# A list schedule that reckons with a transfer rate of 205 GB/s in place of 370 GB/s for all but the first nine DMA transfers of a two-layer encoder

## The chip, the cores and the metric

One core of a Trainium2 chip runs the whole kernel. The metric is the device time of one execution in microseconds, as the median of several executions.

## The reference

The input x (512 tokens by 1024) is layer-normed and goes through two layers. Each layer projects x with w_in (1024 x 4608) into three groups of heads, mixes them with w_out, norms, and then runs a gated MLP with a convolution of width 3. Cut to what matters:

```python
proj = x @ w_in                       # split into da_q, da_k, da_v, hg_q, hg_ff, hg_fb, hg_i, hg_g, mx_q
da_o = rms_norm(diff_attention(dq, dk, dv, lam), da_norm_g)          # 4 heads
hg_o = rms_norm(o_fwd + o_bwd, hg_norm_g) * silu(hg_g)               # gated linear recurrence, 4 heads
mx_o = memory_attention(mx_q, mem @ w_mem_kv)                        # 256 memory tokens, 4 heads
x = layer_norm(ALPHA * x + concat(da_o, hg_o, mx_o) @ w_out)
u = depthwise_conv_centred(x @ w_up, conv_w, conv_b)                 # 2 x 2816 channels
gate, val = split(u)
x = layer_norm(ALPHA * x + (silu(gate) * val) @ w_down)
```

All inputs and weights are float32.

## The kernel before

**Weights.** Every weight goes through `prep` in pieces of 1 MB, 122 in all. A piece is loaded by SyncE into a staging tile `wst` (two buffers); ScalarE squares it and sums (L307); TensorE adds the sums over the partitions in a matmul of one column (`stat`, L168); three small VectorE instructions make a power-of-two scale from it (L155, L157, L159); ScalarE writes the float16 high part `wh` (L310), VectorE the float16 low part `wl` (L311). `wh` and `wl` have four buffers each. After L311 the staging buffer is free for the next load. For w_up a piece is two loads of 512 KB (L300), for the others one load of 1024 KB (L302).

**Matmuls.** Every product is made of three float16 matmuls (high x high, high x low, low x high) in `mm` (L140), so one piece feeds 48 matmuls of 512 columns, but half as much for w_mem_kv, where there are 256 memory tokens. The PSUM tiles of the projections are called mm (two buffers) and sc (three), those of transposes and of small sums tr (two).

**The MLP.** The 22 pairs of gate and value columns are worked in groups of 2, 4, 4, 4, 4 and 4. A pair is 48 matmuls (mm: gate, sc: value), then for each half a ScalarE instruction out of PSUM (L1147) and two VectorE ones for the convolution (L1148, L1149), then the SiLU (L1150) and the product on GpSimd (L1151), which writes a quarter of the group's tile t. When the group is whole, `split_group` squares it on ScalarE (L536), sums it by a matmul of one column (`gss`, L168) and splits it into float16 high and low parts (L545, L547). While that happens TensorE multiplies the group before with w_down (`down`, with its results added to z by VectorE in L569). This place, where a group ends, is called a boundary below.

**The planner.** The instructions are first traced without an order. `make_plan` then makes one: `extract` gives each a cost in microseconds and its predecessors, `deadlines` a due time counted back from TensorE's program order (through buffer reuse too), and `simulate` runs a list schedule: on each engine the instruction that is ready first goes next, and of several ready ones the one with the earliest due time. Which instruction uses which buffer follows from the same simulation. The plan is then frozen: the kernel is built a second time with every engine's queue in exactly this order and with these buffers. The chip does not choose; each engine takes its queue from the front, and an instruction that waits holds up all behind it.

In `simulate` a transfer holds the memory for its bytes over `DMA_RATE`, one transfer after the other, and lands `DMA_LAT` = 2.1 us on top of that. In `deadlines` a load is due its bytes over `DMA_RATE` plus 2 us before its first reader. The first nine transfers of the program (`FIRST`: the constants, two rows of the first norm's vectors, four tiles of x, two weight pieces) get due times that put them ahead of everything.

Of the kernel before, what the change touches and what calls it, by code (L numbers as in the profile page):

```python
# [1205 lines left out]

LAT = 0.055
DMA_LAT = 2.1
DMA_RATE = 370e3


def _esize(dt):
# [72 lines left out]
def extract(instrs):  # L1285
    ops = []
    last_half = None
    for i in instrs:
# [3 lines left out]
        o = Op()  # L1292
# [96 lines left out]
    for o in ops:  # L1389
        for p in o.preds:  # L1390
            ops[p].succs.append(o.i)
    run = []
    for o in ops + [None]:
        if o is not None and o.eng != "PE":
# [12 lines left out]
def simulate(ops, tiles, prio, fixed=None, wait=0.0, log=None):  # L1407
# [65 lines left out]
    while done < N:  # L1473
# [42 lines left out]
        if o.dmab:  # L1516
            free[e] = t + o.cost
            d0 = max(dma_free, t + 0.3)
            dma_free = d0 + o.dmab / DMA_RATE
            end[i] = dma_free + DMA_LAT - 0.3  # L1520
# [25 lines left out]

PEN = 20.0
FIRST = 9


def deadlines(ops, tiles):
# [23 lines left out]
    for i in range(N - 1, -1, -1):  # L1575
        o = ops[i]
        d = T[i] if o.eng == "PE" else 1e9 if succ[i] else t
        for s in succ[i]:
            x = D[s] - o.cost - o.tail - LAT
            if o.dmab:  # L1580
                x -= o.dmab / DMA_RATE + 2
            d = min(d, x)
        D[i] = d
    for k, o in enumerate([o for o in ops if o.dmab][:FIRST]):
        D[o.i] = k - 1000.0
# [3 lines left out]
def make_plan(instrs):  # L1589
    ops, tiles = extract(instrs)  # L1590
    _, _, _, order, slot_of = simulate(ops, tiles, deadlines(ops, tiles))
    return list(order.values()), {tiles[t].source_name: s for t, s in slot_of.items()}
# [45 lines left out]
```

## Time and profile before

| what | us |
|---|---|
| median of 3 executions | 1530.62 (1529.3 to 1532.16) |
| the profiled execution, its own time | 1531.11 |
| its span | 1529.3 |
| TensorE busy in it | 1463.1 |
| VectorE busy | 1141.4 |
| ScalarE busy | 861.7 |

The profile is of one execution. Its span runs from the first to the last recorded instruction, and 1.8 us of its own time lie outside. TensorE's busy time is the union of its matmuls as recorded, whose ends are modelled: a matmul of 512 columns is listed with about 380 ns, though in a dense run one starts every 216 ns. A wait in brackets behind an instruction is the idle time of its engine just before it, with what ended it. "SPq" rows are SyncE's queue, which issues the transfers.

### The profile page before, as it was taken

The page shows a single profiled execution, that of the slowest core. Times are in us where ns is not written, and L with a number is a line of the kernel's source. Part 1 is how long each engine was busy: PE and PEld are TensorE (multiplying, and loading weights), DVE is VectorE, ACT ScalarE, POOL GpSimd, SP SyncE. Part 2 cuts the span into 40 slices and gives each one's busy share as a digit, 9 for nine tenths or more (in the row PEclk, how much of TensorE's full clock was granted, in tenths as well). Part 3 has the DMA queues.
Part 4 walks back from the last instruction along what each step waited for, and adds up shares of the span by engine and source line. Part 5 has one row for each costly group of instructions (what it writes and reads, how often), then busy time and mean ns, then how long its engine had stood idle before and what let it go on. Part 6 is the DMA issues. An engine that isn't in the chain of part 4 may idle for free. (4 is left out here: it accounts for less than half of the span.)

```text
span 1529.3 us, 24599 instructions
## 1 busy us (share of the span) xinstructions
PE 1463.1 (96%) x9978; PEld 813.2 (53%) x9978; DVE 1141.4 (75%) x2146; ACT 861.7 (56%) x1092; POOL 231.9 (15%) x250
## 2 busy tenths in 40 slices
PE   6999999998999999999999999999999999999997
PEld 4566575564474444444477476655556444444443
DVE  8998867967897576666685868678788677565767
ACT  6775556664375555545465646565745655545450
POOL 1221303030111000000110321122101101010111
PEclk9999999998999999999999999999999999999999
DMA  6432112212143232332333212121322334223221
GB/s 232 130 127 84 57 56 71 98 59 95 42 138 111 83 111 84 109 111 85 109 111 129 94 34 80 56 75 38 109 83 84 111 96 122 85 83 110 86 80 56
DMA packets 158172, 141.92 MB, mean 93 GB/s; under 512 B 3302, under 2 KB 139114, under 8 KB 158058
## 3 DMA queue, kind: packets, MB, share of 16 engines
q1 hardware_dynamic: 158058, 140.35, 28.2%
q8 instruction: 78, 1.28, 0.3%
q14 instruction: 36, 0.29, 0.1%
HBM read 138.24 MB, written 2.10 MB: 92 GB/s over the span
## 5 line engine op out<-in xcount | busy, mean ns | idle before, releaser
L311 DVE SCALAR_TENSOR_TENSOR wl<-wst,ws,wh 128x2048 f16<-128x2048 f32 x122 | 307.0, 2518 | 100.1 <-ACT wh L310 99.8
L140 PEld LDWEIGHTS <-wh 128*128 128x128 f16 x2624 | 250.8, 98 | 241.8 <-issue 8.1
L307 ACT ACTIVATE wh<-wst 128x2048 bf16<-128x2048 f32 x122 | 232.7, 1908 | 164.9 <-PE stat L168 48.6
L140 PE MATMUL mm<-xl,wh 128*128 128x512 f16 (+1 forms) x832 | 306.3, 368 | 0.0
L140 PE MATMUL mm<-xh,wh 128*128 128x512 f16 (+1 forms) x832 | 306.2, 368 | 0.1
L140 PE MATMUL mm<-xh,wl 128*128 128x512 f16 (+1 forms) x832 | 306.1, 368 | 0.0
L310 ACT ACTIVATE wh<-wst,ws 128x2048 f16<-128x2048 f32 x122 | 243.4, 1996 | 28.8 <-DVE ws L157 14.0
L140 PE MATMUL mm<-wh,t 128*128 128x512 f16 (+1 forms) x768 | 225.4, 370 | 2.7 <-DVE z L569 2.3
L140 PEld LDWEIGHTS <-wl 128*128 128x128 f16 x1312 | 128.5, 98 | 124.8 <-issue 2.3
L140 PEld LDWEIGHTS <-t 128*128 128x128 f16 x1152 | 110.1, 97 | 134.3 <-issue 15.5
L569 DVE SCALAR_TENSOR_TENSOR z<-mm,inv,z 128x512 f32<-128x512 f32 x176 | 129.9, 745 | 47.3 <-PE mm L140 34.3
L1151 POOL TENSOR_TENSOR t<-f 128x512 f32<-128x512 f32 x44 | 66.0, 1500 | 558.3 <-DVE f L1149 282.8
L140 PE MATMUL sc<-xh,wl 128*128 128x512 f16 (+1 forms) x416 | 147.4, 354 | 0.0
L140 PE MATMUL sc<-xl,wh 128*128 128x512 f16 (+1 forms) x416 | 147.4, 354 | 0.0
L140 PE MATMUL sc<-xh,wh 128*128 128x512 f16 (+1 forms) x416 | 147.4, 354 | 0.0
L140 PE MATMUL mm<-wl,t 128*128 128x512 f16 (+1 forms) x384 | 142.0, 370 | 0.0
L155 DVE TENSOR_SCALAR we<-stat 128x1 int32<-128x1 int32 x122 | 18.6, 152 | 94.4 <-PE stat L168 94.0
L140 PE MATMUL mm<-wh,mgh 128*128 128x512 f16 x192 | 73.8, 384 | 12.3 <-DVE z L569 12.3
L1150 ACT ACTIVATE f<-f 128x512 f32<-128x512 f32 x44 | 27.7, 630 | 83.2 <-DVE f L1149 74.6
L140 PE MATMUL mm<-wl,mgh 128*128 128x512 f16 x192 | 74.1, 386 | 0.0
L140 PE MATMUL mm<-wh,mgl 128*128 128x512 f16 x192 | 73.4, 383 | 0.7 <-DVE mgl L547 0.7
L1042 ACT ACTIVATE f<-sc,dam,iqk 128x512 f32<-128x512 f32 x64 | 49.2, 775 | 29.6 <-DVE dam L1040 29.6
(243 smaller groups left out, 2196.3 us busy)
## 6 DMA issues: line engine op xcount, KB each, us to landing
wst<-in_w_up_dram SPq DMA_DIRECT2D x88, 512.0 KB, 4.4
wst<-in_w_in_dram SPq DMA_DIRECT2D x36, 1024.0 KB, 4.9
wst<-in_w_down_dram SPq DMA_DIRECT2D x22, 1024.0 KB, 4.9
wst<-in_w_out_dram SPq DMA_DIRECT2D x12, 1024.0 KB, 4.8
wst<-in_w_mem_kv_dram SPq DMA_DIRECT2D x8, 1024.0 KB, 5.2
z<-in_x_dram SPq DMA_DIRECT2D x4, 512.0 KB, 4.5
mix<-in_ln_g_dram SPq DMA_DIRECT2D x4, 512.0 KB, 3.5
mix<-in_ln_b_dram SPq DMA_DIRECT2D x4, 512.0 KB, 4.8
```

The lines of the kernel that those rows point to most:

```text
L140: T.matmul(o, lhsT, rhs, start=start, stop=stop)
L155: V.tensor_scalar(e, tot.bitcast(I32), 0x7F000000, 1, ALU.bitwise_and, ALU.logical_shift_right)
L307: A.activation(h.rearrange("p a b -> p (a b)").bitcast(BF16), flat, AF.Square, accum_out=ss)
L310: A.activation(h.rearrange("p a b -> p (a b)"), flat, AF.Identity, scale=s)
L311: V.scalar_tensor_tensor(l.rearrange("p a b -> p (a b)"), flat, s, h.rearrange("p a b -> p (a b)"), ALU.mult, ALU.subtract)
L569: V.scalar_tensor_tensor(zs, p_, ivs[half % len(ivs)], zs, ALU.mult, ALU.add)
L1042: A.activation(pe[:, c, :], sc_[c], AF.Exp, bias=mx[:, c : c + 1], scale=iqk, accum_out=z1 if c else z0)
L1150: A.activation(c2[:, 0, :], c2[:, 0, :], AF.Silu)
L1151: G.tensor_tensor(gt[:, n, :], c2[:, 0, :], c2[:, 1, :], ALU.mult)
```

## The change

The planner's rate falls from 370e3 to 205e3 bytes per microsecond, and the sizes of the first nine transfers are scaled by 205/370 beforehand, so that for these the quotient stays what it was. All the others take 1.8 times as long in the plan, in the simulation and in the due times. No instruction is added or taken away; the four queues of the engines, SyncE's order of transfers and the choice of buffers are worked out anew from these numbers.

```diff
 LAT = 0.055
 DMA_LAT = 2.1
-DMA_RATE = 370e3
+DMA_RATE = 205e3
...
     for o in ops:
         for p in o.preds:
             ops[p].succs.append(o.i)
+    for o in [o for o in ops if o.dmab][:FIRST]:
+        o.dmab *= FAST
     run = []
...
 PEN = 20.0
 FIRST = 9
+FAST = 205 / 370.0
```

## Rows read from the trace of the kernel before

**Rows 1.** The page, part 1: busy time of each engine, share of the span, instructions.
```profile
PE 1463.1 (96%) x9978; PEld 813.2 (53%) x9978; DVE 1141.4 (75%) x2146; ACT 861.7 (56%) x1092; POOL 231.9 (15%) x250
```

**Rows 2.** The waits of TensorE over the whole span: who waited for whom, total us, how often, the longest.
```profile
PE mm L140 <- DVE z L569: 14.6, 11, 2.7
PE tr L262 <- DVE z L258: 9.0, 4, 4.9
PE tr L168 <- ACT t L536: 5.5, 4, 1.5
PE stat L168 <- ACT wh L307: 4.0, 7, 1.1
PE sc L140 <- POOL w L817: 3.7, 3, 1.9
```

**Rows 3.** The page, part 6: transfers by tensor, how many, KB each, median us from issue to landing.
```profile
wst<-in_w_up_dram SPq DMA_DIRECT2D x88, 512.0 KB, 4.4
wst<-in_w_in_dram SPq DMA_DIRECT2D x36, 1024.0 KB, 4.9
wst<-in_w_down_dram SPq DMA_DIRECT2D x22, 1024.0 KB, 4.9
```

**Rows 4.** The view of transfers over the first 60 us, in 40 slices of 1.5 us each: GB/s moved.
```profile
GB/s 0 59 251 393 421 398 386 385 387 426 391 410 346 0 0 261 384 172 129 0 30 0 0 136 386 178 57 350 292 0 0 11 0 5 67 357 382 368 206 18
```

**Rows 5.** The waits of SyncE's queue: total us, how often, the longest.
```profile
SPq L302 <- DVE wl L311: 833.0, 72, 28.9
SPq L300 <- DVE wl L311: 334.0, 37, 16.7
```

**Rows 6.** The waits of ScalarE over the whole span: total us, how often, the longest.
```profile
ACT wh L307 <- DMA wst<-in_w_up_dram: 36.4, 18, 4.2
...
ACT wh L307 <- DMA wst<-in_w_down_dram: 18.8, 8, 2.8
...
ACT t L536 <- POOL t L1151: 12.2, 4, 3.6
```

**Rows 7.** The timeline around one boundary in the MLP of the second layer (1338 to 1358 us): start us, duration us, engine, line, operation, out<-in.
```profile
1338.40 3.22 DVE L311 SCALAR_TENSOR_TENSOR wl<-wst,ws,wh 128x2048 f16<-128x2048 f32 x1 [0.35 <-ACT wh L310]
...
1343.40 0.63 ACT L1150 ACTIVATE f<-f 128x512 f32<-128x512 f32 x1 [1.66 <-DVE f L1149]
1345.88 0.17 PE L168 MATMUL stat<-wss,ones 128*128 128x1 bf16 x1
...
1347.01 1.91 ACT L307 ACTIVATE wh<-wst 128x2048 bf16<-128x2048 f32 x1 [2.97 <-DMA wst<-in_w_up_dram]
...
1348.91 0.76 ACT L1147 ACTIVATE f<-sc,cvb,cw 128x512 f32<-128x512 f32 x1
1349.06 0.16 PE L168 MATMUL stat<-wss,ones 128*128 128x1 bf16 x1 [0.61 <-ACT wh L307]
...
1349.58 1.99 ACT L310 ACTIVATE wh<-wst,ws 128x2048 f16<-128x2048 f32 x1
...
1351.69 2.35 DVE L311 SCALAR_TENSOR_TENSOR wl<-wst,ws,wh 128x2048 f16<-128x2048 f32 x1
1351.92 3.24 POOL L1151 TENSOR_TENSOR t<-f 128x512 f32<-128x512 f32 x1 [12.45 <-DVE f L1149]
...
1355.20 1.91 ACT L536 ACTIVATE t<-t 128x2048 bf16<-128x2048 f32 x1 [3.63 <-POOL t L1151]
...
1357.25 0.16 PE L168 MATMUL tr<-gss,ones 128*128 128x1 bf16 x1 [1.48 <-ACT t L536]
```

**Rows 8.** The view of one line, GpSimd's product in the MLP, over the whole span: duration ns min/median/max, first and last start us, shapes.
```profile
L1151 POOL TENSOR_TENSOR t<-f x44: 1264/1272/3304, 445.0 to 1481.6; 128x512 f32<-128x512 f32 x44
```

**Rows 9.** The same view of the low part of a weight on VectorE.
```profile
L311 DVE SCALAR_TENSOR_TENSOR wl<-wst,ws,wh x122: 2322/2351/3350, 19.1 to 1484.4; 128x2048 f16<-128x2048 f32 x122
```

**Rows 10.** Busy time by stretch, the first two of 50 us each and the last of 30 us (the span ends at 1529.3): PE, PEld, DVE, ACT, POOL busy us (instructions), granted clock of TensorE, share of the DMA engines, GB/s.
```profile
0.00:50.00 50.00, 36.05 (x219) 23.45 (x220) 42.69 (x108) 33.26 (x45) 3.88 (x14) 1.00 0.56 199
50.00:100.00 50.00, 47.35 (x592) 32.20 (x591) 44.64 (x97) 38.86 (x47) 11.81 (x9) 1.00 0.45 148
...
1500.00:1530.00 30.00, 19.92 (x93) 8.82 (x90) 22.40 (x36) 0.00 (x0) 6.11 (x8) 0.89 0.19 70
```

**Rows 11.** The timeline between 78 and 88 us, in the first layer's work on w_mem_kv: two L311 and the first matmul on TensorE with a weight of this stage behind each.
```profile
78.16 2.32 DVE L311 SCALAR_TENSOR_TENSOR wl<-wst,ws,wh 128x2048 f16<-128x2048 f32 x1
...
81.63 0.39 PE L140 MATMUL mm<-t,wh 128*128 128x256 f16 x2
...
84.33 2.35 DVE L311 SCALAR_TENSOR_TENSOR wl<-wst,ws,wh 128x2048 f16<-128x2048 f32 x1 [1.24 <-ACT wh L310]
...
87.19 0.28 PE L140 MATMUL mm<-wh,t 128*128 128x256 f16 x1
```

**Rows 12.** Busy time by stretch around 354 to 364 us, where the first layer's w_out stage ends: columns as in rows 10.
```profile
354.00:356.00 2.00, 0.92 (x6) 0.62 (x6) 2.00 (x5) 2.00 (x3) 0.00 (x0) 0.99 0.33 78
356.00:358.00 2.00, 1.26 (x6) 0.23 (x5) 2.00 (x7) 1.96 (x6) 0.00 (x0) 0.50 1.15 345
358.00:360.00 2.00, 2.00 (x8) 0.57 (x5) 2.00 (x3) 0.38 (x2) 0.00 (x0) 0.50 0.38 113
360.00:362.00 2.00, 2.00 (x7) 0.53 (x6) 0.95 (x7) 0.28 (x1) 0.00 (x0) 0.50 0.67 262
362.00:364.00 2.00, 2.00 (x13) 1.42 (x12) 1.53 (x6) 2.00 (x5) 0.00 (x0) 0.80 0.04 11
```

## The prediction

> **What bounds the kernel now.** I read the page's busy times first, then TensorE's waits, then the transfers and who waits for them, and last the timeline wherever TensorE stood still. TensorE is busy for 1463.1 us of 1529.3 [rows 1], so 66.2 us are idle, and no change of order can give more than that. Of these, 16.6 lie in the first 100 us (100 less 36.05 and 47.35) [rows 10], most of it waiting for the first norm, and 9.4 in the last 29.3 us (19.92 busy) [rows 10], where the last norm is stored; the planner can hardly touch either. Some 40 us are left, none of the waits longer than 2.7 us. The named ones [rows 2] are matmuls of the w_out and w_down stages that wait for L569 to empty a PSUM buffer (14.6), the gss matmul that waits for L536 (5.5 in 4), and the stat matmul that waits for L307 (4.0 in 7). None of TensorE's named waits is for a weight's low part, and SyncE sends a load as soon as L311 lets go of a staging buffer: that wait is nearly all its queue does [rows 5]. So transfers don't bound the kernel; the exact order in four in-order queues does.
>
> **Is the new rate the right one?** No. A piece of 1 MB costs the old plan 2.1 + 1.05 MB/370 GB/s = 2.1 + 2.83 = 4.93 us and the chip 4.9 [rows 3]; the opening burst runs at 385 to 425 GB/s [rows 4]. At 205 GB/s the plan reckons 2.1 + 5.11 = 7.21 us, 2.28 too much. A single half piece of w_up (4.4 [rows 3]) lies between the two plans' 3.5 and 4.7, but its second half follows at once: in [rows 7] an L311 that ends at 1341.6 frees the buffer, and ScalarE has the whole new piece at 1347.0, 5.4 us later with the issue. The change thus puts 2.28 us of slack behind each of some 120 loads. The Trainium skill, page "DMA: Bandwidth & Descriptors", section "Anatomy of one DMA — SWDGE (gpsimd) path", fits 2.0 us plus bytes over 436 GB/s to transfers that GpSimd issues; an estimate by that page is 4.4 us for 1 MB, the rows' 4.9 decides for these, and by the page the surplus would be 2.8 instead of 2.3, which speaks against the new rate as a description.
>
> **What the slack changes in the queues.** A due time only decides between instructions that are ready together, and a load is ready when its buffer is, which SyncE waits for anyway [rows 5]; so SyncE's order stays nearly the same, and so do the first nine loads. What moves is L307 on ScalarE. In the plan it is ready 2.28 us later, and whatever becomes ready in between goes ahead of it. The stat matmul on TensorE moves back with it. On the chip the data still come after 4.9 us, so neither is late for that reason.
>
> **Term 1, the stat matmul.** The old order, in which the data land just in time, leaves ScalarE idle before L307 for 36.4 + 18.8 us in 26 cases of the MLP [rows 6], and when the real landing is a little late, TensorE stands behind the stat matmul: 7 times, 4.0 us, 1.1 at most [rows 2]. All are shorter than 2.28, so a stat matmul that is planned 2.28 us later on TensorE finds its sum ready. I take -4.0 (bounds -4.0 and 0, where the matmul keeps its place for want of other work between). Late next is gss.
>
> **Term 2, the boundary.** The timeline of one boundary [rows 7] shows the whole chain. The last pair's sums are in PSUM at 1345.9, but the next in ScalarE's queue is L307, which waits 2.97 us for its load until 1347.01 and takes 1.91 more. L1147 behind it runs at 1348.91 instead of 1346; after it come the convolution, the SiLU, the product on GpSimd, L536 and gss, for which TensorE waits 1.48. With the slack, L1147 is ready some 2 us before L307 in the plan and goes first: 2.9 us gained in the chain of this boundary, more than the 1.48. Against that stands the product: it takes 3.24 us here beside an L311 [rows 7], where its median is 1.27 [rows 8] and the plan reckons about 1.4. L1147 first lets L310 of the older piece go next and L311 behind it, and L311 can meet the product again. Then 1.9 us of lateness remain, which alone would make the 1.48. I take half of the four waits, -2.7 (bounds -5.5 and 0). L311 is itself drawn out, 3.22 us [rows 7] against a median of 2.35 [rows 9]. The Trainium skill, page "GPSIMD Engine Reference", section "1. Specifications", says that GpSimd's access to SBUF is shared with VectorE, with contention beside instructions of two SBUF inputs; L311 is one, and the two durations in the rows agree. By that rule this term would be 0 and the sum 2.7 higher.
>
> **Term 3, the start.** Between 20 and 95 us each load is used almost as soon as it is ready: L311 ends at 80.48 and the next weight matmul starts at 81.63, another ends at 86.68 and TensorE uses it at 87.19 [rows 11], while VectorE is busy 42.69 and 44.64 of 50 us [rows 10]. Here w_mem_kv feeds only half as many matmuls per piece. An L307 that is queued later ends later, L311 too, and the staging buffer is reloaded later; nothing in VectorE's queue has room to make it good. What covers it is other matmuls (the recurrence), and where they run out TensorE waits. The price lies between 0 (cover holds) and two reuses of one buffer in this stretch, 2 x 2.28 = 4.6. I take 1.1, half of one reuse, as the rows show 0.5 to 1.2 us between the weight and its use and TensorE nearly always occupied.
>
> **Term 4, the rest.** The waits for L569 (14.6), for the recurrence's operands (3.7 for L817) and for norms [rows 2] are dealt out anew. No row gives a direction, so I take 0. For the bounds I take the dearest place that a wait of this kind now has: after a stretch in which TensorE was busy 0.92 and 1.26 of 2 us, its granted clock stands at 0.50, the 1.2 GHz level, from about 356 to 362.5 [rows 12]. Work done there takes twice as long, so some 6.5 us at that level cost about 3.3. One such fall more or less is -3.3 to +3.3.
>
> **Sum.** -4.0 - 2.7 + 1.1 + 0 = -5.6. The profiled execution took 1531.11, so its successor takes 1525.5; that execution stands 0.5 above the median of 1530.62, so the median comes to 1525.0.
>
> **Rivals.** *Nothing to measure.* The boundary keeps its waits because product and L311 meet (term 2 is 0), the start costs one whole reuse (+2.3), and two boundaries that now pass without a wait get the 1.48 (+3.0): -4.0 + 2.3 + 3.0 = +1.3, about 1532. The difference of 1.97 us between the product beside L311 and alone speaks for it (the rule of the Trainium skill under term 2 describes this case); that 8 of 12 boundaries have no gss wait now, though most have an L311 near, speaks against. That the change hardly does what it says belongs here too: if ScalarE has nothing else ready in the 2.28 us, the queues come out as they were, and the time is 1530.6. ScalarE's idle 36.4 us before L307 say that this is often so, but rows 7 that it isn't at the places that cost.
>
> *Slower: the weights of the start come late.* In the first 100 us, and again in the second layer's w_mem_kv and w_in pieces, the plan believes that two staging buffers give a piece only every 7 to 8 us and lets other work in front of L307. On the chip that work then really delays the reload, and the delay adds up over two reuses: +4.6, without gains at the boundaries, which makes 1535.2. It decides from the point at which TensorE's idle time in the first 100 us goes above some 20 us (16.6 now) and the waits name L310 or L311. For it: VectorE's load and the narrow margins of rows 10 and 11. Against: none of the costly waits names a weight today, and TensorE has the recurrence's matmuls to do.
>
> **How the numbers follow.** The forecast, 1525.0, has a chance of 0.50; nothing to measure 0.23; slower 0.27. Forecast's own range: 1520 (both terms whole, no cost at the start: -9.5 from 1530.6 is 1521, with part of a fall of the clock) to 1527.5. The whole range goes down to 1530.6 - 9.5 - 3.3, about 1518, and up to the slower case's 1535.2 with part of a fall of the clock, 1537. A measurement of this kernel can tell about 0.2%, 3.1 us, from no change; faster means below 1527.6, slower above 1533.7. Faster 0.50, same 0.23, slower 0.27.
>
> **What would show it.** Right: in TensorE's waits the line of stat behind L307 falls from 4.0 to under 1, the line of gss behind L536 from 5.5 to about 2.8; ScalarE's wait for w_up and w_down loads falls from 55 to under 30; at the boundaries L1147 of the last pair stands ahead of the L307 that waits for a load. Load durations stay at 4.9. Wrong: the idle time in the first 100 us grows by more than 4, the waits for L569 grow by more than the 6.7 of terms 1 and 2, or the clock stands at its lower level for longer in sum than before. I would be most wrong if the order of TensorE's own work (attention between projections) changes widely, for then the 40 us of small waits are dealt anew and term 4 outweighs the others.

## The result and the profile after

The changed kernel takes 1512.24 us (median of 4, 1509.85 to 1514.96) where the kernel before takes 1530.89 in the same comparison (median of 4): 0.988 times as long, 95% interval 0.986 to 0.990, or 18.6 us less. The forecast was 5.6 less. The profiled execution took 1512.29, with a span of 1510.5, so between the two profiled executions 18.8 us are gone.

The page, part 1 (busy time of each engine), and from part 6 the transfers, tensor by tensor, with the median from issue to landing:

```profile
PE 1458.8 (97%) x9978; PEld 816.0 (54%) x9978; DVE 1155.0 (76%) x2146; ACT 861.3 (57%) x1092; POOL 219.8 (15%) x250
...
wst<-in_w_up_dram SPq DMA_DIRECT2D x88, 512.0 KB, 4.6
wst<-in_w_in_dram SPq DMA_DIRECT2D x36, 1024.0 KB, 4.8
wst<-in_w_down_dram SPq DMA_DIRECT2D x22, 1024.0 KB, 4.9
```

The transfers are within 0.2 us of [rows 3]: what changed is not their length but what the plan believes of it. TensorE's idle time fell from 66.2 to 51.7 us (1510.5 less 1458.8). GpSimd lost 12.1 us of busy time and VectorE gained 13.6 with the same instructions [rows 1]; where most of that lies comes below.

TensorE's waits over the whole span, the longest sums first:

```profile
PE mm L140 <- DVE z L569: 9.2, 8, 2.7
PE tr L262 <- DVE z L258: 8.9, 4, 4.7
...
PE sc L140 <- DVE t L813: 2.6, 1, 2.6
...
PE tr L168 <- ACT mgh L536: 1.3, 1, 1.3
...
PE sc L140 <- POOL w L817: 0.6, 1, 0.6
```

Against [rows 2] the line of stat behind L307 (4.0) and the line of gss behind L536 (5.5) are gone altogether; the wait for L569 fell from 14.6 to 9.2, and sc behind L817 from 3.7 to 0.6. ScalarE's waits for transfers, over the whole span:

```profile
ACT wh L307 <- DMA wst<-in_w_up_dram: 12.5, 5, 2.7
ACT wh L307 <- DMA wst<-in_w_in_dram: 11.0, 2, 10.8
ACT wh L307 <- DMA wst<-in_w_mem_kv_dram: 2.2, 1, 2.2
```

L307 waited 55.2 us for w_up and w_down in 26 cases [rows 6]; now it is 12.5 in 5, and w_down isn't in the list. SyncE's queue still waits for L311, now 795.1 and 361.6 us (compare [rows 5]).

The timeline of the boundary that [rows 7] shows, now at 1332 to 1342 us:

```profile
1334.74 0.17 PE L168 MATMUL stat<-wss,ones 128*128 128x1 bf16 x1
1334.94 0.78 ACT L1147 ACTIVATE f<-sc,cvb,cw 128x512 f32<-128x512 f32 x1 [2.05 <-PE stat L168]
...
1335.62 1.99 ACT L310 ACTIVATE wh<-wst,ws 128x2048 f16<-128x2048 f32 x1
1337.44 1.27 POOL L1151 TENSOR_TENSOR t<-f 128x512 f32<-128x512 f32 x1 [9.12 <-DVE f L1149]
1337.51 1.90 ACT L307 ACTIVATE wh<-wst 128x2048 bf16<-128x2048 f32 x1
1338.23 2.63 DVE L311 SCALAR_TENSOR_TENSOR wl<-wst,ws,wh 128x2048 f16<-128x2048 f32 x1
...
1339.41 1.90 ACT L536 ACTIVATE t<-t 128x2048 bf16<-128x2048 f32 x1
...
1341.70 0.17 PE L168 MATMUL tr<-gss,ones 128*128 128x1 bf16 x1
```

The last pair's L1147 now stands ahead of L307 and starts 0.20 us after the stat matmul; before, it stood behind an L307 that waited 2.97 us for its load, and started 3.03 after. The product L1151 comes 2.50 us after L1147 and takes 1.27, where it took 3.24. From the stat matmul at the head of these rows to gss it is 6.96 us in place of 11.37, and gss waits for nothing.

The most telling view is the windows from one last pair's product to the next (columns: window, its length, then busy us and instruction count for TensorE, weight loads, VectorE, ScalarE and GpSimd, granted clock, share of the DMA engines, GB/s). Before:

```profile
1351.92:1416.92 65.00, 62.81 (x297) 28.25 (x296) 40.55 (x64) 33.69 (x32) 7.04 (x4) 1.00 0.31 98
1416.92:1481.64 64.72, 62.82 (x297) 28.31 (x296) 40.11 (x63) 33.69 (x32) 7.06 (x4) 1.00 0.30 98
```

After:

```profile
1337.44:1399.78 62.34, 62.34 (x297) 28.32 (x296) 41.96 (x63) 33.66 (x33) 5.08 (x4) 1.00 0.33 102
1399.78:1462.12 62.34, 62.34 (x297) 28.32 (x296) 41.72 (x61) 33.65 (x33) 5.09 (x5) 1.00 0.31 102
```

A group of four pairs has the same 297 matmuls in both, and after the change TensorE does them without a gap: 62.34 us, where 288 large ones at 216 ns would be 62.2. Before it took 65.00. Of the 2.66 us gained, 2.19 were idle time in the record (0.61 for stat, 1.48 for gss, 0.10 in smaller gaps), and 0.47 were not seen: the same matmuls are listed as 62.81 us busy instead of 62.34, because the record gives the last matmul before a stall its 380 ns and not the 216 of its pace.

### The profile page after: what moved, and what is told of

Its sections match the earlier page's. It is cut to its first block, busy times and chain, and to the rows that moved or that the text cites. A ratio compares the mean times of both kernels' runs of the same rounds, so it can differ in the third digit from the quotient of the medians.

```text
span 1510.5 us, 24589 instructions
## 1 busy us (share of the span) xinstructions
PE 1458.8 (97%) x9978; PEld 816.0 (54%) x9978; DVE 1155.0 (76%) x2146; ACT 861.3 (57%) x1092; POOL 219.8 (15%) x250
## 3 DMA queue, kind: packets, MB, share of 16 engines
q8 instruction: 78, 1.28, 0.3%
## 5 line engine op out<-in xcount | busy, mean ns | idle before, releaser
L311 DVE SCALAR_TENSOR_TENSOR wl<-wst,ws,wh 128x2048 f16<-128x2048 f32 x122 | 315.9, 2590 | 68.2 <-ACT wh L310 67.8
L307 ACT ACTIVATE wh<-wst 128x2048 bf16<-128x2048 f32 x122 | 232.2, 1904 | 116.0 <-PE stat L168 53.2
L310 ACT ACTIVATE wh<-wst,ws 128x2048 f16<-128x2048 f32 x122 | 243.5, 1996 | 41.5 <-DVE wi L159 23.0
L569 DVE SCALAR_TENSOR_TENSOR z<-mm,inv,z 128x512 f32<-128x512 f32 x176 | 129.8, 745 | 46.0 <-PE mm L140 32.4
L1151 POOL TENSOR_TENSOR t<-f 128x512 f32<-128x512 f32 x44 | 56.0, 1272 | 549.2 <-DVE f L1149 450.0
L155 DVE TENSOR_SCALAR we<-stat 128x1 int32<-128x1 int32 x122 | 18.6, 152 | 120.8 <-PE stat L168 120.5
L1147 ACT ACTIVATE f<-sc,cvb,cw 128x512 f32<-128x512 f32 x44 | 34.1, 776 | 75.8 <-PE stat L168 72.2
```

Source lines behind the costliest of these rows:

```text
L155: V.tensor_scalar(e, tot.bitcast(I32), 0x7F000000, 1, ALU.bitwise_and, ALU.logical_shift_right)
L307: A.activation(h.rearrange("p a b -> p (a b)").bitcast(BF16), flat, AF.Square, accum_out=ss)
L310: A.activation(h.rearrange("p a b -> p (a b)"), flat, AF.Identity, scale=s)
L311: V.scalar_tensor_tensor(l.rearrange("p a b -> p (a b)"), flat, s, h.rearrange("p a b -> p (a b)"), ALU.mult, ALU.subtract)
L569: V.scalar_tensor_tensor(zs, p_, ivs[half % len(ivs)], zs, ALU.mult, ALU.add)
L1147: A.activation(c, p_, AF.Identity, scale=cw[:, 1, v : v + 1], bias=cvb[:, l, i + 22 * v : i + 22 * v + 1])
```

## The experiments

The theories were these. S: the slack moves L307 behind other ScalarE work, above all behind the last pair's L1147 at the MLP's boundaries. D: the due times do it. Q: loads that are planned longer queue differently behind each other. R: the queues are dealt out anew and came out well by luck. A: the gain is spread over all loads in proportion. G: GpSimd's product, which the plan reckons at 1.39 us and the chip at 3.24 when it meets L311, is what lengthens the boundary. Each run was compared with runs of the kernel before on the same chip (1531.2 to 1532.6 us).

**e1: the simulation alone.** From the changed kernel, with 370 GB/s left in the due times.

```diff
-                x -= o.dmab / DMA_RATE + 2
+                x -= o.dmab / 370e3 + 2
```

> 205 GB/s in the simulation alone, due times as with 370. Theory S (slack in the simulated landing puts L307 behind other ScalarE work): about the changed kernel's 1512, within 4. Theory D (earlier due times of the loads do it): about 1531. Theory R (any new plan deals the waits anew, and this one was lucky): anywhere from 1515 to 1540.

Measured 1512.02, ratio 0.987 [0.984, 0.989]. All of the gain; the lines of stat and of gss are gone here too.

**e2: the due times alone.** The kernel before, with 205 GB/s only there.

```diff
-                x -= o.dmab / DMA_RATE + 2
+                x -= o.dmab / 205e3 + 2
```

> 205 GB/s in the due times alone, simulation as with 370. S: about 1531 within 4, with the stat and gss waits of TensorE still there (together 7 us or more). D: about 1512. R: anywhere from 1515 to 1540.

Measured 1525.90, ratio 0.996 [0.995, 0.997]. TensorE's waits:

```profile
PE mm L140 <- DVE z L569: 7.1, 9, 1.5
PE stat L168 <- ACT wh L307: 5.8, 8, 2.5
PE tr L168 <- ACT t L536: 5.7, 5, 1.5
```

The boundary's waits stay, and D falls as the cause. Of the median 6.7 us are gone all the same, a little more than S allows. The profiled execution was the slowest of the ten (1530.41); its trace has half of the waits for L569 (7.1 against 14.6 [rows 2]), but more for stat (5.8 against 4.0). About half of the 6.7 goes with a higher granted clock, as said at the end of this section.

**e3: latency in place of rate.** The kernel before; a load behind the first nine keeps its 370 GB/s on the memory and lands later by the difference of the two quotients.

```diff
-            end[i] = dma_free + DMA_LAT - 0.3
+            end[i] = dma_free + DMA_LAT - 0.3 + (0.0 if i in first else o.dmab * (1 / 205e3 - 1 / 370e3))
```

> The memory is held as at 370 GB/s and the due times are as before, but each load after the first nine lands later by what 205 would add (2.28 us for 1 MB), so transfers don't queue up longer. S: 1510 to 1516, stat and gss waits at 0. If it is the queueing of transfers in the plan that counts (theory Q): within 5 of 1531. R: anywhere from 1515 to 1540.

Measured 1513.44, ratio 0.987 [0.985, 0.989]; no wait of stat for L307, and of the gss waits, which S had put at 0, one of 1.4 us, at the first layer's first boundary. Q falls: that loads line up behind each other in the plan plays no part.

**e4: ten loads.** The kernel before, with the longer transfer only for those pieces whose L307 the plan puts directly ahead of an L1147 that reads an sc tile (the last pair of a group). The plan is made again until there is no such place; 10 of 122 pieces are marked.

```diff
+SC = 1147
...
+        ahead = [ops[p] for p, q in zip(act, act[1:]) if ops[p].line == 307 and ops[q].line == SC and any(t.startswith("sc") for t in ops[q].tiles)]
...
+        for o in new:
+            o.dmab *= 370 / 205
```

> Rate 370 everywhere, but for the pieces whose L307 stood directly ahead of the convolution's L1147 out of an sc tile on ScalarE (10 of 122 pieces, found in the plan itself) the simulated transfer takes 370/205 as long. Due times as before. S: the boundaries of the MLP bring some 13 of the 18.6 us, 1518 within 3, stat and gss waits near 0. R: 1531 within 8. If the gain were spread over all loads (theory A): 1529, a tenth of it.

Measured 1519.83, ratio 0.9915 [0.9893, 0.9936]: 12.8 us, where the change gave 18.6 and e1 20.6, from ten loads. The gss waits are gone and one stat wait of 0.7 is left; the waits for L569 (13.9) are nearly as before, so they are no part of it.

**e5 and e6: the loads of the MLP alone, and all but these.** The kernel before, with loads made longer by tensor.

```diff
+    for o in [o for o in ops if o.dmab][FIRST:]:
+        if any(x in o.order_ins[0].tensor.name for x in ("w_up", "w_down")):
+            o.dmab *= 370 / 205.0
```

(e6 has `if not any`.)

> The plan has the longer transfers (205 GB/s) for the loads of w_up and w_down alone; all other loads keep 370. If the slack at the six boundaries of the two MLPs is the main cause (S), the stat and gss waits vanish here and the time is 1517 to 1521, as with the ten loads chosen by hand. If every kind of load contributes in proportion to its number (A), w_up and w_down are about half of the transfers and the time is 1521 to 1524. If the queues are merely dealt out anew and came out well by chance (R), the time lies anywhere from 1510 to 1532, with no tie to the boundaries.

> The reverse: the longer transfers for all the loads behind the first nine but w_up and w_down. S expects the waits at the MLP boundaries to remain (stat about 4, gss about 5.5) and the time to fall only by what e4 left over, about 6: 1524 to 1528. A expects 1521 to 1524 as in the run before. A start that is planned too late (the cost in term 3) should show here too, as about +1 at 240 us.

Measured 1517.99 (0.9895 [0.986, 0.993]) and 1527.99 (0.9968 [0.995, 0.998]): 14.4 and 4.4 us less than 1532.36. Together 18.7, as much as the whole change, though e5's interval alone runs from 11 to 22 us. A falls, for both runs lie outside the 1521 to 1524 that it asks for. In e6 the last pair's L1147 still stands behind a waiting L307 (its timeline at the same boundary):

```profile
1343.23 1.91 ACT L307 ACTIVATE wh<-wst 128x2048 bf16<-128x2048 f32 x1 [2.76 <-DMA wst<-in_w_up_dram]
...
1345.14 0.76 ACT L1147 ACTIVATE f<-sc,cvb,cw 128x512 f32<-128x512 f32 x1
...
1347.92 2.34 DVE L311 SCALAR_TENSOR_TENSOR wl<-wst,ws,wh 128x2048 f16<-128x2048 f32 x1
1348.14 3.24 POOL L1151 TENSOR_TENSOR t<-f 128x512 f32<-128x512 f32 x1 [12.24 <-DVE f L1149]
...
1353.48 0.16 PE L168 MATMUL tr<-gss,ones 128*128 128x1 bf16 x1 [1.48 <-ACT t L536]
```

The stall of gss is the same to the hundredth. What e6 does gain is in its waits: L569 9.9 in place of 14.6 and L817 0.9 in place of 3.7. In e5 these stay at 13.8 and 3.7, while gss is gone and 0.7 of stat is left. So the change has two separate parts, and the larger one is the boundary. One expectation was missed: the late start that was to show in e6 as +1 near 240 us isn't there, the row at 263.66 us comes 0.98 earlier than in the kernel before. More on this under term 3.

**e7 and e8: other rates.** The changed kernel with another number: 420 and 320 GB/s for all but the first nine.

```diff
-DMA_RATE = 205e3
+DMA_RATE = 420e3
...
-FAST = 205 / 370.0
+FAST = 420 / 370.0
```

> The rate for the others goes up to 420 instead of down: loads are planned 0.3 us shorter than they are. Four of the boundary places still have an L307 that waits for its load directly ahead of the last pair's L1147 in the plan. S expects the boundary waits to remain there and 1526 to 1534. R expects no tie: anywhere from 1510 to 1532.

> A small slack: 320 GB/s for all but the first nine, some 0.44 us more for 1 MB. In the plan no last pair's L1147 stands behind a waiting L307 any more. If what counts is the order at these places and not the size of the slack (S), the stat and gss waits are gone and the time is 1515 to 1522. If the size counts (the slack must cover the waits of up to 1.5 us), most of the waits remain and the time is 1525 or more.

Measured 1532.10 (1.000 [0.998, 1.002]) and 1517.22 (0.9895 [0.987, 0.992]). At 320 the slack for 1 MB is only 0.44 us, less than each of the gss waits (1.05 to 1.48), and still all of them are gone, with 0.7 us of stat waits left. The slack needn't cover the wait; it need only turn the order of two instructions in the plan. At 420 the time is what S expected, but the waits aren't:

```profile
PE stat L168 <- ACT wh L307: 9.5, 11, 1.3
...
PE tr L168 <- ACT t L536: 1.0, 1, 1.0
```

In its trace an L307 that waits for its load stands directly ahead of the last pair's L1147 at two of the twelve boundaries, where the kernel before has five, and the gss waits fell from 5.5 to 1.0; what they gave back is lost in more stat waits (4.0 before) and ahead of the first MLP, whose first transposes (L288) come 3.9 us later. So the order at the boundaries doesn't settle the time alone. What speaks against R is the row of runs: each kernel with slack for the MLP's loads (the change, e1, e3, e4, e5, e8, e12) is 12.8 to 20.6 us faster, except e11 below with its late start, and none without it by more than 7.1.

**e9: another product.** The kernel before with its own plan; in the second layer L1151 multiplies by one number per partition. This changes what is computed there. Its cost in the plan is held.

```diff
-            G.tensor_tensor(gt[:, n, :], c2[:, 0, :], c2[:, 1, :], ALU.mult)
+            G.tensor_scalar(gt[:, n, :], c2[:, 0, :], c2[:, 1, 0:1], None, ALU.mult) if l == 1 else G.tensor_tensor(gt[:, n, :], c2[:, 0, :], c2[:, 1, :], ALU.mult)
...
+            if o.eng == "POOL" and o.line == 1151:
+                o.cost, o.tail = 1.3864, 0.0
```

> The kernel before with its own plan and the same queues, but in the second layer L1151 multiplies by one number per partition (the first column of the other factor) instead of by the other factor whole: the product reads one stream of SBUF instead of two, and the computed product is another one. Its cost in the plan is held at the old value, so nothing moves. If the drawn-out product (3.24 us beside L311, 1.27 alone) is what lengthens the last three boundaries (G), L1151 falls to 1.5 us or less there, the three gss waits of the second layer (about 4) vanish and the time falls by 4 to 6: 1526 to 1528. If L307 ahead of L1147 is the loss and the product only rides on it (S), the time falls by 0 to 3 and the stat waits stay.

Measured 1527.76, ratio 0.998 [0.996, 1.000]. The edit failed at its purpose: the product didn't get shorter beside L311 but longer. Its timeline at the same boundary:

```profile
1353.19 2.35 DVE L311 SCALAR_TENSOR_TENSOR wl<-wst,ws,wh 128x2048 f16<-128x2048 f32 x1
1353.44 3.53 POOL L1151 TENSOR_SCALAR t<-f 128x512 f32<-128x512 f32 x1 [11.54 <-DVE f L1149]
...
1359.05 0.16 PE L168 MATMUL tr<-gss,ones 128*128 128x1 bf16 x1 [1.78 <-ACT t L536]
```

It still tells something. The product is 0.29 us longer than 3.24 and gss waits 0.30 longer than 1.48: the wait follows the product one to one. The 1.97 us that L311 adds to it are thus more than the 1.48 of the wait. The median fell by 3.4 all the same, and the trace shows where. The second layer's MLP, the only place with the other product, takes 369.1 us from its first transpose (L288) to the last matmul, where it took 372.1: its stat waits are gone (1.7 before, against S), L569 holds TensorE up for 2.8 us in place of 4.5, and only gss waits longer (4.9 in place of 4.0). That the profiled execution (1532.47) is no faster as a whole comes mostly from a stretch ahead of this MLP in which the granted clock fell to 0.50, the 1.2 GHz level, for 6.8 us, after 4 us with TensorE busy for 2.13; in the kernel before, 1.99 of 4 at the same place, it didn't. Before, then e9 (window, length, TensorE busy, granted clock, DMA share, GB/s):

```profile
1090.00:1120.00 30.00, 26.72 (x165) 1.00 0.26 88
1090.00:1120.00 30.00, 26.72 (x143) 0.89 0.27 88
```

A likely reason for the gain, not tested: where the new product comes first it draws L311 out less (2.64 us in place of 3.2), so a staging buffer is free some 0.6 us earlier.

**e10: the product's true price.** The rate stays at 370; the plan reckons 3.25 us for L1151.

```diff
+            if o.eng == "POOL" and o.line == 1151:
+                o.cost = 3.25
```

> The rate stays at 370 for all loads; the plan reckons 3.25 us for L1151 instead of 1.39. If the wrong price of the product was the fault (G), the plan now finds an order in which nobody waits for it: gss waits gone and 1517 to 1523. S expects that gss is only placed later behind other matmuls, that L307 still stands ahead of the last pair's L1147 at four or five of the boundaries, and the time falls by no more than the gss waits, 0 to 6: 1526 to 1532.

Measured 1524.02, ratio 0.995 [0.993, 0.997], between the two theories, and the trace says why: each holds in one layer. In the first layer a waiting L307 stands ahead of the last pair at three boundaries (two before), and at two of them the product still meets L311; the timeline of one:

```profile
668.92 1.91 ACT L307 ACTIVATE wh<-wst 128x2048 bf16<-128x2048 f32 x1 [2.92 <-DMA wst<-in_w_up_dram]
...
670.83 0.76 ACT L1147 ACTIVATE f<-sc,cvb,cw 128x512 f32<-128x512 f32 x1
...
673.61 2.34 DVE L311 SCALAR_TENSOR_TENSOR wl<-wst,ws,wh 128x2048 f16<-128x2048 f32 x1
673.84 3.24 POOL L1151 TENSOR_TENSOR t<-f 128x512 f32<-128x512 f32 x1 [12.40 <-DVE f L1149]
...
680.98 0.17 PE L168 MATMUL tr<-gss,ones 128*128 128x1 bf16 x1
```

Here gss is only placed later, it waits for nothing, and the layer gains next to nothing: its first product came 1.03 us later than before (446.07 against 445.04), and of two rows behind the layer one (803.79 us before) comes 1.29 later, the other (809.06) 0.34 earlier. In the second layer L1147 goes first at the last three boundaries, the product takes 1.27, and from 1283 to 1471 us the kernel gains 7.1 (L1151 went from 3.23 ahead of its old place to 10.30). The gss wait can thus be hidden with hardly any gain; it is the shorter chain that pays.

**e11 and e12: more slack, and slack for the first nine too.** The changed kernel with 150 GB/s for all but the first nine; and the kernel before with 205 for all, which is the change without its exception.

```diff
-DMA_RATE = 205e3
+DMA_RATE = 150e3
...
-FAST = 205 / 370.0
+FAST = 150 / 370.0
```

```diff
-DMA_RATE = 370e3
+DMA_RATE = 205e3
```

> Twice the slack of the change: 150 GB/s for all but the first nine, 4.2 us too much for 1 MB instead of 2.3. If the order at the boundaries is all that matters (S), the order there is the same and the time stays within 4 of the changed kernel: 1508 to 1516. If too much slack makes loads really late (the rival of the start), weights are used later than they could be and the time rises to 1518 or more, with more TensorE waits behind L307, L310 or L311.

> The change without its exception: 205 GB/s for all transfers, the first nine too. If the exception protects the start, as term 3 reckons the price of late pieces, the first 240 us get 2 to 5 us longer than in the changed kernel and the time is 1514 to 1518. If the start hangs on the first norm and not on the plan's order of these nine, the time stays within 2 of the changed kernel: 1510 to 1514.

Measured 1526.45 (0.997 [0.995, 0.998]) and 1514.84 (0.9885 [0.987, 0.990]). With 150 most of the gain is lost, though the boundary is as good as after the change. TensorE's waits of e11 in the first 160 us:

```profile
PE mm L140 <- DVE wl L311: 4.5, 4, 1.7
...
PE mm L140 <- ACT wh L310: 1.4, 2, 0.8
```

These two are new: TensorE waits for weights that are split too late. A ScalarE row of the recurrence (L744) that stood at 159.53 us comes 12.0 later (1.6 in the changed kernel), one that stood at 263.66 comes 6.6 later (1.3), and the granted clock of 50 to 100 us is 0.93 (0.97 after, 1.00 before). The rival "the weights of the start come late" is this, at nearly twice the slack. Without the exception for the first nine (e12) the first of these rows comes 4.2 later in place of 1.6, as the first theory said, but the intervals of e12 and of the changed kernel overlap; by the medians the exception is worth 2.6 us.

One number tells a boundary that is held up from one that isn't: the window from the product of the second layer's last pair near 1340 us to that of the next group, as in the fences above, with TensorE's busy time in it.

| kernel | L307 directly ahead of L1147 there | window, us | TensorE busy | median, us |
|---|---|---|---|---|
| before | yes | 65.00 | 62.81 | 1530.89 |
| e6, all but the MLP's loads | yes | 65.29 | 62.83 | 1527.99 |
| e9, other product | yes | 64.78 | 62.82 | 1527.76 |
| e7, 420 | no | 63.70 | 62.61 | 1532.10 |
| e10, dear product | no | 62.76 | 62.49 | 1524.02 |
| e8, 320 | no | 62.50 | 62.50 | 1517.22 |
| e4, ten loads | no | 62.34 | 62.34 | 1519.83 |
| e11, 150 | no | 62.34 | 62.34 | 1526.45 |
| after | no | 62.34 | 62.34 | 1512.24 |

In e1, e3, e5 and e12 it is 62.34 as well, in e2 64.90. The window doesn't order the medians: e7 has a shorter one than the kernel before and no gain, and kernels with 62.34 lie between 1512 and 1526 us, by what happens elsewhere. None of the runs is clearly faster than the changed kernel; e1's median is 0.2 us lower, well inside its interval.

The medians also carry a second thing, the granted clock. Its mean differs from execution to execution; on the chip of e1 to e4 the kernel before took 1536.07 us at 0.988 and 1528.74 at 0.996. A straight line through the executions of the kernel before on each chip gives about 1.0 to 1.1 us for 0.001. Held against that line, so at equal clock, the gains are as an estimate 20.5 us for e1, 3.4 for e2, 18.1 for e3, 14.2 for e4, 15.2 for e5, 3.9 for e6, 12.6 for e8, 2.9 for e9, 7.7 for e10, 6.6 for e11, 16.7 for e12, and e7 is 1.5 slower. Most change little. In e2 half of the gain goes: nine of its ten executions had 0.994 to 0.996, the profiled one 0.992, the median of the kernel before. Whether the order of e2 brings that clock isn't shown.

## Why the prediction was wrong in size

The direction, the place and the mechanism of the larger part were right; the sum was 13 us short. By e5 and e6, three steps make that up: the halving in term 2 (some 2.8 us), the bound that terms 1 and 2 share (9.5 where e5 gave 14.4, so 4.9), and term 4, put at nothing (5.5, with term 3). With e5's wide interval these shares are rough. By the steps:

- *Is the new rate the right one?* No, as forecast: loads still take 4.9 us, and e3 shows that another form of pessimism in the simulation does the same.
- *What the slack changes in the queues.* Right: L1147 ahead of L307 at the boundaries, and e1 and e2 confirm that the simulation's order does it and not the due times.
- *Term 1, stat, -4.0.* Right: the line is gone.
- *Term 2, the boundary, -2.7.* This is the step whose reasoning failed. I halved the waits because "L311 can meet the product again". It does meet it, but the other way round. Which of the two starts first decides who pays. In the kernel before, its own timeline had both cases; here the one behind a pair that isn't held up, just ahead of the first L311 of [rows 7]:

```profile
1338.19 1.28 POOL L1151 TENSOR_TENSOR t<-f 128x512 f32<-128x512 f32 x1 [1.89 <-DVE f L1149]
```

  L311 starts 0.21 us after this product and takes 3.22; the product keeps its 1.28. At the four boundaries with a gss wait L311 starts 0.17 to 0.23 *before* the product, and the product takes 3.24 to 3.30. After the change the product starts 0.79 before L311 at 1337.44. L311 pays 0.28 and nobody waits for L311. Over the whole span L1151 takes 56.0 us in place of 66.0 and L311 315.9 in place of 307.0: most of what GpSimd lost and VectorE gained. I read the 3.22 of L311 as the same meeting without asking who came first; the answer stood one row away. So the whole of the 5.5 was to be had, not half.
- *The bound itself was too low.* Terms 1 and 2 whole are 9.5, the MLP's loads alone gave 14.4 (e5). Part of the difference is in the windows: a boundary cost 2.66 where its named waits showed 2.09. Summing named waits left out what the record hides in the listed length of the last matmul; the period of a group against 288 matmuls of 216 ns, 65.0 against 62.2, would have shown it. The rest of the difference, some 2 us in e5, I haven't traced to rows.
- *Term 3, the start, +1.1.* The number came out, but as far as shown by luck. The rows of the recurrence come 1.6 us later at 159.53 and 1.3 at 263.66. But in e5, where the loads of the start are planned as before, the first of them comes 1.5 later too; and in e1 and e6, where they are planned as long as in the changed kernel, it comes 0.8 and 0.7 *earlier*. What the two late kernels share is a fall of the granted clock to 0.50 for 3.4 us between 70 and 79 us (in the changed kernel after 65 to 70 us with TensorE busy for 3.08 of 5). The windows of the first 100 us in the changed kernel, to be held against [rows 10], and TensorE from 50 to 100 us in e5, e1 and e6, in this order:

```profile
0.00:50.00 50.00, 35.98 (x218) 23.82 (x219) 42.85 (x102) 32.63 (x45) 3.87 (x14) 1.00 0.56 199
50.00:100.00 50.00, 47.21 (x526) 32.08 (x524) 42.62 (x96) 35.77 (x42) 14.69 (x9) 0.97 0.38 127
...
50.00:100.00 50.00, 47.35 (x523) 0.97 0.45 148
50.00:100.00 50.00, 46.94 (x591) 1.00 0.39 127
50.00:100.00 50.00, 47.19 (x605) 1.00 0.38 127
```

  So no run shows, apart from the clock, that weights planned later cost anything at the start with this slack; with nearly twice as much they do (e11). TensorE's idle time of the first 100 us is 16.8 (16.6 before), and the rival's point of 20 isn't reached.
- *Term 4, the rest, 0.* Off by about 5.5: e6, the loads outside the MLP, gives -4.4 where terms 3 and 4 together said +1.1. The waits for L569 and L817 that e6 loses (4.7 and 2.8) have the same cause as the boundary, loads that the plan believes to be just in time. I had called them dealt out anew without direction. That cause is argued from e6's waits; no run takes a single one of them apart. The falls of the clock, which gave the bounds, cancelled out: the mean granted clock of the two profiled executions is 0.992 in both.
- *The rivals.* "Nothing to measure" rested on the meeting of product and L311, and falls with term 2: they do hold each other up, as that rival said, but L311 pays for it. "Slower" is real but needs more slack: e11 shows it at 150 GB/s.

How the boundary's gain splits between L307's wait and the drawn-out product, e9 was meant to show and couldn't. One boundary of the kernel before does in part, in the first layer:

```profile
601.75 1.91 ACT L307 ACTIVATE wh<-wst 128x2048 bf16<-128x2048 f32 x1 [3.50 <-DMA wst<-in_w_up_dram]
...
603.80 0.16 PE L168 MATMUL stat<-wss,ones 128*128 128x1 bf16 x1 [1.14 <-ACT wh L307]
...
606.66 1.27 POOL L1151 TENSOR_TENSOR t<-f 128x512 f32<-128x512 f32 x1 [12.98 <-DVE f L1149]
607.09 2.99 DVE L311 SCALAR_TENSOR_TENSOR wl<-wst,ws,wh 128x2048 f16<-128x2048 f32 x1
...
611.51 0.17 PE L168 MATMUL tr<-gss,ones 128*128 128x1 bf16 x1
```

L307 waits here longer than at the others, but other work on ScalarE and VectorE (L381, L382) puts off L310 and L311, the product starts first, and gss waits for nothing; only stat waits. So a late L307 alone costs stat's wait, and the gss wait stands only where the product is drawn out as well: at all four other boundaries of the kernel before at which an L307 waits. Still open are the rest of e5's gain and what brings the higher clock in e2.

## What to carry to other kernels

Where a plan freezes in-order queues, a cost that is believed exactly true puts an instruction that waits for a transfer at the front just as the transfer lands, and everything behind it pays for a real delay; a small pessimism on such costs turns the order, and here 0.44 us of it gave most of the gain (e8), while 4.2 us, nearly twice what the change has, made the weights late (e11). To size such a change, don't add up the named waits: take the period of a repeated stage and hold it against its matmuls at their pace. And where two engines meet and one of them is drawn out, look for which of them started first before deciding who will pay after the change.

## What the runs showed of the hardware

GpSimd's 128x512 float32 product and VectorE's L311 (two float32 or float16 operands of 128x2048 in SBUF) don't run side by side at full speed: the one that starts second pays. With L311 first by 0.23 us the product ends 1.12 us after L311's end (1354.04 to 1355.16 in the kernel before), nearly its whole length of 1.27. With the product first by 0.21 us, L311 takes 3.2 in place of 2.34; first by 0.43, 3.0; first by 0.79, 2.6: it pays for what is left of the product. That the product reads one stream in place of two doesn't help it: 1.56 alone, 3.53 beside L311, 1.97 more, as with two streams (e9). But it spares L311, which takes 2.64 us there when it starts 0.19 behind the product, not 3.2. VectorE's instructions that read PSUM (L569) kept their 0.74 to 0.75 us beside the product.
